# Huber loss on one core: other tile widths, other load pieces, and seven small loads ahead of tile 1

## The chip, the cores and the metric

The kernel runs on 1 core of one Trainium2 chip. The metric is the device time of one execution in microseconds (us). Before the change the median of 3 runs is 1868.01 us (1867.77 to 1872.63). A difference of about 0.3% (5.6 us) is what a measurement of this kernel can tell from no change.

## The reference

Two float32 arrays of 8192 x 8192 go in, one comes out. Every element is computed by itself:

```python
diff = pred - target
abs_diff = np.abs(diff)
return np.where(abs_diff <= 1.0, 0.5 * diff**2, abs_diff - 0.5)
```

The kernel computes it without a branch: with d the difference and c = d clipped to [-1, 1], the result is the larger of c*c/2 and |d| - 0.5. Where |d| is at most 1, the first is at least as large as the second; elsewhere the first is 0.5 and the second is larger.

## The kernel before

The arrays are taken flat and cut into tiles. One tile is a contiguous stretch of 128 times `width` elements, laid over 128 partitions, so that each partition's row is `width` contiguous elements in the memory. There are 524,288 columns to cover. Before the change they are cut into a first tile of 7,616 columns and 39 of W = 13,248, 40 tiles (n = 40) in all.

Four buffers in the on-chip memory hold whole tiles: `a0` and `a1` for `pred`, `b0` and `b1` for `target`. Tile i uses the buffers numbered i mod 2, and the result is made in place in the b buffer and stored from there. So a load of tile i + 2 into a b buffer has to wait until the store of tile i has landed, and a load into an a buffer until the compute of tile i is through with it.

All transfers are issued by one engine, SyncE (SP), in program order, and each is carried by up to 16 DMA engines, which work through what SP has issued. The order is written out by hand: load tile 0, load tile 1, and then for each i compute tile i, store tile i, load tile i + 2. When an instruction on SP waits, all that stands behind it on SP waits as well. Completions are told by eight DMA semaphores taken in turn, so a DMA can also wait for the one that stands eight before it.

`load` (lines 49 to 65) loads most tiles with one DMA for a and one for b. Tiles 0, 1, n-3 and n-2 are loaded in halves, and the last tile in quarters in an order of its own. `store` (67 to 70) stores a tile with one DMA, the last tile with five. `compute` (72 to 100) cuts a tile into pieces: two for tile 0, three of 4,416 columns for most tiles, four for the last but one, eight for the last. Each piece goes through five steps: VectorE subtracts (line 92) and clips (93), ScalarE squares (96) and takes the absolute value (97), and VectorE subtracts 0.5 and takes the larger (86), up to two pieces later.

Of the kernel before, what the change touches and what calls it, by code (L numbers as in the profile page):

```python
# [1 line left out]

# [4 lines left out]

@with_exitstack
def kernel(  # L10
    ctx: ExitStack,
    tc: tile.TileContext,
    pred: bass.AP,
    target: bass.AP,
    out: bass.AP,
):
    nc = tc.nc
    P = 128
    fp32 = mybir.dt.float32
    Alu = mybir.AluOpType  # L20
    Act = mybir.ActivationFunctionType
    SQRT_HALF = 0.70710678118654752

    total = pred.shape[0] * pred.shape[1] // P
    W = 13248
    H, Q, E = W // 2, W // 4, W // 8

    widths = [W] * (total // W)
    if total % W:
        widths.insert(0, total % W)  # L30
    n = len(widths)
    starts = [sum(widths[:i]) * P for i in range(n)]

    def block(x, i):
        flat = x.rearrange("r m -> (r m)")
        return flat[starts[i] : starts[i] + P * widths[i]].rearrange("(p m) -> p m", p=P)

    pool = ctx.enter_context(tc.tile_pool(name="slots", bufs=1))
    a_slots = [pool.tile([P, W], fp32, name=f"a{k}") for k in range(2)]
    b_slots = [pool.tile([P, W], fp32, name=f"b{k}") for k in range(2)]  # L40

    def cuts(pieces):
        at, found = 0, []
        for w in pieces:
            found.append(slice(at, at + w))
            at += w
        return found

    def load(i):
        a, b = a_slots[i % 2], b_slots[i % 2]  # L50

        def get(dst, src, c):
            nc.sync.dma_start(out=dst[:, c], in_=block(src, i)[:, c])  # L53

        if i == n - 1:
            c = cuts([Q] * 4)
            order = [(0, 0), (0, 1), (1, 0), (1, 1), (0, 2), (1, 2), (0, 3), (1, 3)]
            for which, k in order:
                get((a, b)[which], (pred, target)[which], c[k])
            return  # L60
        w = widths[i]
        pieces = [w // 2] * 2 if i in (0, 1, n - 3, n - 2) else [w]
        for c in cuts(pieces):
            get(a, pred, c)
            get(b, target, c)

    def store(i):
        pieces = [Q] * 3 + [E] * 2 if i == n - 1 else [widths[i]]
        for c in cuts(pieces):
            nc.sync.dma_start(out=block(out, i)[:, c], in_=b_slots[i % 2][:, c])  # L70

    def compute(i):
        if i == n - 1:
            pieces = [E] * 8
        elif i == n - 2:
            pieces = [Q] * 4
        elif i == 0:
            pieces = [widths[0] // 2] * 2
        else:
            pieces = [W // 3] * 3  # L80
        todo = []

        def finish(keep):
            while len(todo) > keep:
                a, b = todo.pop(0)
                nc.vector.scalar_tensor_tensor(  # L86
                    out=b, in0=a, scalar=-0.5, in1=b, op0=Alu.add, op1=Alu.max
                )

        for c in cuts(pieces):  # L90
            a, b = a_slots[i % 2][:, c], b_slots[i % 2][:, c]
            nc.vector.tensor_tensor(out=a, in0=a, in1=b, op=Alu.subtract)  # L92
            nc.vector.tensor_scalar(  # L93
                out=b, in0=a, scalar1=-1.0, scalar2=1.0, op0=Alu.max, op1=Alu.min
            )
            nc.scalar.activation(out=b, in_=b, func=Act.Square, scale=SQRT_HALF)  # L96
            nc.scalar.activation(out=a, in_=a, func=Act.Abs)  # L97
            todo.append((a, b))
            finish(2)
        finish(0)  # L100

    ctx.enter_context(tc.manual_schedule())

    load(0)
    load(1)
    for i in range(n):
        compute(i)
        store(i)
        if i + 2 < n:
            load(i + 2)  # L110

# [1 line left out]
_INS = ['pred', 'target']  # L114
_OUTS = [((8192, 8192), 'float32')]

# [23 lines left out]
```

## Time and profile before

| | |
|---|---|
| median of 3 runs | 1868.01 us |
| the profiled execution's own time | 1869.17 us |
| its span | 1867.4 us |
| VectorE (DVE) busy | 1406.2 us, 75% |
| ScalarE (ACT) busy | 903.9 us, 48% |
| DMA queue that SP issues, share of 16 engines | 99.9% |
| bytes moved, mean rate | 805.37 MB, 431 GB/s |
| a load or store of 13,248 columns | 6,624 KB |

The profile shows one execution. The span is what the trace covers, and the execution's own time is a little longer. Busy times are summed per engine. "GB/s" is given for 40 equal slices of the span, 46.7 us each. The queue "q1 hardware_dynamic" is the one that carries all loads and stores; its share of 99.9% says that on average all 16 DMA engines had a packet in hand throughout. A packet is one row of one transfer, carried by one engine, or the 4 bytes with which an engine tells that its part of a transfer is done. In lines of waits, "SPq L53 <- DMA out_dram<-b" reads: SP's queue, at an instruction of line 53, waited for a transfer from a b buffer to the output; then follow total us, times, and the longest. In lines of stretches the columns are the stretch, its length, each engine's busy time with its instructions, the TensorE clock (not used here), the DMA share and GB/s.

### The profile page before, as it was taken

The page shows a single profiled execution, that of the slowest core. Times are in us where ns is not written, and L with a number is a line of the kernel's source. Part 1 is how long each engine was busy: PE and PEld are TensorE (multiplying, and loading weights), DVE is VectorE, ACT ScalarE, POOL GpSimd, SP SyncE. Part 2 cuts the span into 40 slices and gives each one's busy share as a digit, 9 for nine tenths or more (in the row PEclk, how much of TensorE's full clock was granted, in tenths as well). Part 3 has the DMA queues.
Part 4 walks back from the last instruction along what each step waited for, and adds up shares of the span by engine and source line. Part 5 has one row for each costly group of instructions (what it writes and reads, how often), then busy time and mean ns, then how long its engine had stood idle before and what let it go on. Part 6 is the DMA issues. An engine that isn't in the chain of part 4 may idle for free.

```text
span 1867.4 us, 994 instructions
## 1 busy us (share of the span) xinstructions
DVE 1406.2 (75%) x375; ACT 903.9 (48%) x251; POOL 0.2 (0%) x4
## 2 busy tenths in 40 slices
DVE  5677777777777777777777777777777777777886
ACT  3444444444444444444444444444444444444454
POOL 0000000000000000000000000000000000000000
DMA  9999999999999999999999999999999999999999
GB/s 412 423 432 436 436 431 433 436 432 431 428 435 434 435 432 432 432 435 434 434 434 435 432 434 432 435 434 432 436 434 432 434 434 432 432 436 430 432 429 390
DMA packets 19879, 805.37 MB, mean 431 GB/s; under 512 B 2208, under 2 KB 2208, under 8 KB 2464
## 3 DMA queue, kind: packets, MB, share of 16 engines
q1 hardware_dynamic: 19872, 805.32, 99.9%
q14 instruction: 7, 0.06, 0.0%
HBM read 536.87 MB, written 268.44 MB: 431 GB/s over the span
## 4 chain that ended last, share of the span: by engine, by line
DMA 61%; DVE 37%; issue 0%; SPq 0%; DVEq 0%
DMA b<-in_target_dram 33%; DMA out_dram<-b 28%; DVE b L86 15%; DVE a L92 15%; DVE b L93 8%; SPq L53 0%; DVEq L136 0%; DVEq L92 0%
## 5 line engine op out<-in xcount | busy, mean ns | idle before, releaser
L96 ACT ACTIVATE b<-b 128x4416 f32<-128x4416 f32 (+3 forms) x125 | 461.1, 3688 | 945.6 <-DVE b L93 945.6
L92 DVE TENSOR_TENSOR a<-a,b 128x4416 f32<-128x4416 f32 (+3 forms) x125 | 565.4, 4523 | 439.2 <-DMA b<-in_target_dram 439.2
L86 DVE SCALAR_TENSOR_TENSOR b<-a,b 128x4416 f32<-128x4416 f32 (+3 forms) x125 | 558.6, 4521 | 2.7 <-ACT a L97 2.7
L97 ACT ACTIVATE a<-a 128x4416 f32<-128x4416 f32 (+3 forms) x125 | 460.3, 3682 | 0.0
L93 DVE TENSOR_SCALAR b<-a 128x4416 f32<-128x4416 f32 (+3 forms) x125 | 293.1, 2344 | 4.3
L96 ACT ACT_TABLE_LOAD x1 | 1.3, 1283 | 0.7 <-PEq L125 0.7
L125 POOL MEMSET const-bfloat16-1.0<- 128x1 bf16 x1 | 0.1, 102 | 0.0
L125 POOL MEMSET const-uint8-127<- 128x1 uint8 x1 | 0.1, 101 | 0.0
L125 POOL MEMSET const-float32-0.0<- 128x1 f32 x1 | 0.1, 99 | 0.2 <-issue 0.2
L125 POOL MEMSET const-float32-1.0<- 128x1 f32 x1 | 0.1, 98 | 0.0
## 6 DMA issues: line engine op xcount, KB each, us to landing
out_dram<-b SPq DMA_DIRECT2D x38, 6624.0 KB, 26.9
a<-in_pred_dram SPq DMA_DIRECT2D x35, 6624.0 KB, 42.1
b<-in_target_dram SPq DMA_DIRECT2D x35, 6624.0 KB, 31.3
a<-in_pred_dram SPq DMA_DIRECT2D x6, 3312.0 KB, 30.4
b<-in_target_dram SPq DMA_DIRECT2D x6, 3312.0 KB, 30.5
a<-in_pred_dram SPq DMA_DIRECT2D x4, 1656.0 KB, 31.6
b<-in_target_dram SPq DMA_DIRECT2D x4, 1656.0 KB, 18.6
out_dram<-b SPq DMA_DIRECT2D x3, 1656.0 KB, 18.9
```

Source lines behind the costliest of these rows:

```text
L86: nc.vector.scalar_tensor_tensor(out=b, in0=a, scalar=-0.5, in1=b, op0=Alu.add, op1=Alu.max)
L92: nc.vector.tensor_tensor(out=a, in0=a, in1=b, op=Alu.subtract)
L93: nc.vector.tensor_scalar(out=b, in0=a, scalar1=-1.0, scalar2=1.0, op0=Alu.max, op1=Alu.min)
L96: nc.scalar.activation(out=b, in_=b, func=Act.Square, scale=SQRT_HALF)
L97: nc.scalar.activation(out=a, in_=a, func=Act.Abs)
L125: nc = _bacc.Bacc("TRN2", target_bir_lowering=False, num_devices=1)
```

## The change

Four things change.

1. The tile widths. The remainder of 7,616 columns and one full tile are pooled and halved: tile 0 and the last tile have 10,432 columns each, the 38 tiles between them 13,248.
2. The loads of the last tiles. Tile n-3 is loaded whole. Tile n-2 is loaded in pieces of three quarters of a, half of b, one quarter of a, half of b. The last tile takes six loads instead of eight: three quarters of a, then three quarters of b one by one, then the last quarter of a and of b. Tiles 0 and 1 are loaded in halves as before.
3. The pieces of the last tile's compute (eighths) and stores (three quarters and two eighths) stay in number; they shrink with the tile.
4. Seven loads are added among those of tile 0. They read 14, 12, 10, 8, 6, 4 and 2 rows of the first 3,072 columns of tile 1 of `pred` into `a1`, one row out of every eight. Two of them follow the first half of a of tile 0, two the first half of b, three the second half of a. The first load of tile 1 writes the same bytes again later. The number of rows is also the number of DMA engines that such a load is spread over.

On SP, the ninth DMA (the load of 4 rows) now waits for the first one, the tenth and eleventh for the second and third, and the twelfth, the first load of tile 1, for all added loads.

```diff
-    H, Q, E = W // 2, W // 4, W // 8
 
-    widths = [W] * (total // W)
-    if total % W:
-        widths.insert(0, total % W)
+    ends = total % W + W
+    widths = [ends - ends // 2] + [W] * (total // W - 1) + [ends // 2]
...
+    HALVES = (("a", 0, 1), ("b", 0, 1), ("a", 2, 3), ("b", 2, 3))
+    LOADS = {
+        0: HALVES,
+        1: HALVES,
+        n - 2: (("a", 0, 2), ("b", 0, 1), ("a", 3, 3), ("b", 2, 3)),
+        n - 1: (("a", 0, 2), ("b", 0, 0), ("b", 1, 1), ("b", 2, 2), ("a", 3, 3), ("b", 3, 3)),
+    }
+    PARTS = {0: 2, n - 2: 4, n - 1: 8}
...
-    load(0)
-    load(1)
+    def load_all(i):
+        for piece in LOADS.get(i, (("a", 0, 3), ("b", 0, 3))):
+            load(i, *piece)
+
+    EXTRA = 3072
+    later = [14, 12, 10, 8, 6, 4, 2]
+
+    def ahead(count):
+        for _ in range(count):
+            k, r = later[0], len(later)
+            rows = slice(r, r + 8 * (k - 1) + 1, 8)
+            nc.sync.dma_start(
+                out=a_slots[1][rows, :EXTRA], in_=block(pred, 1)[rows, :EXTRA]
+            )
+            later.pop(0)
+
+    for piece, count in zip(LOADS[0], (2, 2, 3, 0)):
+        load(0, *piece)
+        ahead(count)
+    load_all(1)
     for i in range(n):
         compute(i)
         store(i)
         if i + 2 < n:
-            load(i + 2)
+            load_all(i + 2)
```

A piece such as `("a", 0, 2)` names the buffer and the first and last quarter of the tile's columns that the load covers.

More of the change, by code (lines that the diff above doesn't have):

```diff
@@ L40 @@
     b_slots = [pool.tile([P, W], fp32, name=f"b{k}") for k in range(2)]
[L42 to L53, printed above, removed]
-        if i == n - 1:
[L56 to L65, printed above, removed]
@@ L67, in store, with shares, load @@
-    def store(i):
-        pieces = [Q] * 3 + [E] * 2 if i == n - 1 else [widths[i]]
-        for c in cuts(pieces):
+    def shares(i, parts):
+        w = widths[i] // parts
+        edges = [k * w for k in range(parts)] + [widths[i]]
+        return [slice(edges[k], edges[k + 1]) for k in range(parts)]
+    def load(i, which, first, last):
+        quarters = shares(i, 4)
+        c = slice(quarters[first].start, quarters[last].stop)
+        dst, src = (a_slots, pred) if which == "a" else (b_slots, target)
+        nc.sync.dma_start(out=dst[i % 2][:, c], in_=block(src, i)[:, c])
@@ new lines, with store @@
+    HALVES = (("a", 0, 1), ("b", 0, 1), ("a", 2, 3), ("b", 2, 3))
[6 more added lines that the diff above has]
+    PARTS = {0: 2, n - 2: 4, n - 1: 8}
+    def store(i):
+        if i == n - 1:
+            eighths = shares(i, 8)
+            pieces = [slice(eighths[k].start, eighths[k + 1].stop) for k in (0, 2, 4)]
+            pieces += eighths[6:]
+        else:
+            pieces = shares(i, 1)
+        for c in pieces:
@@ L70, in store @@
             nc.sync.dma_start(out=block(out, i)[:, c], in_=b_slots[i % 2][:, c])
     def compute(i):
[L73 to L80, printed above, removed]
         todo = []
@@ L88, in finish @@
                 )
-        for c in cuts(pieces):
+        for c in shares(i, PARTS.get(i, 3)):
             a, b = a_slots[i % 2][:, c], b_slots[i % 2][:, c]
```

## The prediction

> **What bounds the kernel now.** I read the page's busy shares first, then its DMA lines, then SP's waits, then the rate by stretches, and last the single DMA packets in the trace's records.
>
> ```profile
> DVE 1406.2 (75%) x375; ACT 903.9 (48%) x251; POOL 0.2 (0%) x4
> ...
> GB/s 412 423 432 436 436 431 433 436 432 431 428 435 434 435 432 432 432 435 434 434 434 435 432 434 432 435 434 432 436 434 432 434 434 432 432 436 430 432 429 390
> DMA packets 19879, 805.37 MB, mean 431 GB/s; under 512 B 2208, under 2 KB 2208, under 8 KB 2464
> ...
> q1 hardware_dynamic: 19872, 805.32, 99.9%
> ```
>
> The 16 DMA engines are busy for 99.9% of the span, VectorE for 75%, ScalarE for 48%. The rate is level from the third slice to the last but one; only the first and last slices are low. So transfers bound this kernel, and a saving in compute is worth nothing as long as the queue holds work.
>
> ```profile
> SPq L53 <- DMA out_dram<-b: 1000.0, 38, 32.8
> SPq L70 <- DVE b L86: 786.8, 44, 30.8
> ```
>
> The queue that issues everything, SP's, spends nearly the whole span waiting. It waits while transfers issued earlier are still moving, so these waits are cover, not loss: what counts is whether an engine runs dry before SP issues again.
>
> ```profile
> 0.00:25.00 25.00, 9.65 (x3) 7.39 (x3) 0.20 (x4) 1.00 0.95 396
> 49.00:52.00 3.00, 0.00 (x0) 3.00 (x2) 0.00 (x0) 1.00 1.17 397
> 1200.00:1250.00 50.00, 38.53 (x10) 25.81 (x7) 0.00 (x0) 1.00 1.00 434
> 1860.00:1868.00 8.00, 0.00 (x0) 0.00 (x0) 0.00 (x0) 1.00 0.42 173
> ```
>
> The last two columns are the DMA share and GB/s. From 49 to 52 us the engines are fully busy and yet move 397 GB/s instead of 434: packets there take longer. The packet records give the rest. The first packet starts at 1.73 us, the last ends at 1866.06. A row of 52,992 B takes 1956 ns, of 26,496 B 982, of 15,232 B 568, of 13,248 B 495; each engine's share of a DMA closes with a 4-byte packet of 9 ns. With each packet at the shortest time seen for its size, the mean engine needs 1858.6 us; it has 1865.3. Of the 6.7 us between, 3.1 are a few ns on each packet, 0.65 are the first packets of all, and 3.0 are packets that ran over 100 ns long. These 3.0 us lie almost all before 470 us (0.74 at 50 us, 0.45 at 90, 0.57 at 467), mostly at the change from the end of a target load to a store.
>
> Beside this stands the spread of the engines, read off the 16 completions of each DMA: 0.65 us between first and last until 44 us, 1.2 at 156, 2.0 at 297, 3.4 at 501, 3.7 at 1439. Once the engines are over 3 us apart the long packets nearly stop: 0.37 us after 470, against 2.62 between 4 and 470. At the very end it costs: the last engine finishes at 1866.06 and the mean one about 1863.4, so 2.6 us go to the slowest.
>
> **The sum is made against the profiled execution**, 1869.17 us (span 1867.4, 1.8 around it), 1.2 above the median of 1868.01; I add the same change to the median.
>
> **Added bytes.** 14+12+10+8+6+4+2 = 56 rows of 3,072 columns, 12,288 B each: 0.69 MB. Between the 495 ns of 13,248 B and the slope to 568 ns for 15,232 B, a row costs 460 ns and its completion 9. A load of k rows runs on k engines by the change's own words; if these are always the same first ones, two engines carry seven rows (3.3 us), the next two six, and so on to none for the last two. Mean 56 x 0.469 / 16 = +1.6 us. No trace of before shows which engines; were the seven loads on rotating engines, each would carry 1.6.
>
> **Fewer pieces.** DMAs go from 138 to 134 beside the added ones. By the packet sizes, a DMA costs an engine eight rows with some 5 ns each beyond its bytes and one 9 ns completion, of which 3 overlap: four fewer are 4 x (40 + 6) ns, -0.2 us. The bytes of inputs and output are the same.
>
> **The phase of the engines.** The added rows set the engines 0 to 3.3 us apart within the first 30 us, the spread that before reaches after 370 to 470 us. Bounds: at most the 2.62 us of long packets between 4 and 470 us go; at least nothing, and a loss is not excluded, because a pair of engines shares each step. I take -2.0, as the stretch from 300 to 470 us, with 2.0 to 3.0 us of spread, still shows some 1.0 us of long packets, and after 470 they are rare.
>
> **The end.** The last engine is the one that counts. A spread of 3.3 us laid out evenly puts the last 1.65 above the mean, and with the 0.65 us of the start and some drift about 2.3; before has 2.6. I take -0.3; bounds -1.0 (the spread stays as laid out) and +2.0 (natural lag falls on the engines with seven rows).
>
> **The start, covered.** SP now waits: the ninth DMA (4 rows) waits for the first, the tenth and eleventh for the second and third, and the twelfth, the first load of tile 1, for all added rows, since it overwrites them. Behind the twelfth on SP stand the other three loads of tile 1, the store of tile 0 and everything else; VectorE waits for them. A row of 20,864 B takes 775 ns by the slope between 568 and 982, so a half load takes 6.2 us. The first lands near 9 us; the ninth to eleventh are out by about 11, with two half loads (12.4 us) still ahead of the engines. An engine with seven rows finishes the last of them at 2.0 + 0.65 + 3 x 6.2 + 3.3 = 24.6 us. The trace has 0.42 to 0.57 us from a load's last completion packet to the waiting instruction, and 1.0 us from the start of the first issue to the first packet: the twelfth's packets come at about 26.1. An engine with no added rows runs dry at 2.0 + 0.65 + 4 x 6.2 = 27.4. Cover 1.3 us, cost nothing. Were it gone, the engines that stand are those that are 3.3 us ahead, so up to that nothing reaches the end.
>
> **First store, covered.** Tile 0 is 10,432 wide, two pieces of 5,216. Rows by shape give VectorE 4126 ns at 3,808 and 4754 at 4,416, so 5.6 us at 5,216; the scaling goes to 2.9, an activation to 4.5. The last half lands near 31.3; VectorE's subtract and clip (5.6 + 2.9), ScalarE's two (9.0) and the last VectorE step (5.6) end at 54.6. Tile 1's 31.4 us of loads keep the most advanced engine busy until 58.8. Cover some 3 us net of the issue; before had over 10.
>
> **The tail, covered.** Before, VectorE ends its last tile at 1852.5 and transfers run until 1866.06. The last tile shrinks from 13,248 to 10,432 columns, and eight pieces of 1,304 at 4.65 x 1304/1656, about 3.7 us, take 30 instead of 37. Counted from the landing of the store before it, the loads of the last tile keep the queue for 24.6 us, the next store for 15.6, and the last piece is due at 51.0, or 47.7 on the most advanced engine; compute starts at 12.3 and ends at 42.3. Cover some 4 us after the issue; cost nothing.
>
> Sum: +1.6 - 0.2 - 2.0 - 0.3 = **-0.9 us**: span 1866.5, profiled 1868.3, median 1867.1.
>
> [...] The packet records price a DMA's completion at 9 ns on each engine, and 138 DMAs leave the engines 99.9% busy. [...]
>
> **Rivals.**
> 1. *The added rows are simply paid.* The long packets come from something that the phase does not cure, such as the memory's own state early on: all 16 engines are hit at 467 us with 3 us of spread already there, which speaks for it; that they fade as the spread grows speaks against. Then +1.6 - 0.2 + 1.7, by which the two engines with seven rows stand above the mean, = +3.1: 1871.1.
> 2. *The queue runs dry at the start (slower).* Place: the twelfth DMA. The point from which it decides is 3.3 + 1.3 = 4.6 us of delay beyond my 26.1: if the seven loads were each issued only on the landing of the one before, at 0.5 + 1.0 = 1.5 us per round, 10.5 us in all, then 10.5 - 4.6 = 5.9 us stand open, with 3.1 for the paid rows +9.0: 1877.0. For it: the cover of 1.3 is the thinnest of all. Against: each of SP's waits is for a DMA eight back.
> 3. *Reads and writes mixed across the engines slow them.* If each change of direction ran 3.3 us at 397 instead of 434 GB/s, three changes in each of 39 tiles cost 117 x 3.3 x 0.085 = 33 us: 1901. Against: from 500 us on the engines already are 3.4 to 3.7 us apart, at 434.
> 4. *Much faster.* Even with every early long packet gone and all engines ending together the gain is 2.6 + 2.6 + 0.2 - 1.6 = 3.8: 1864.2, short of 0.3%.
>
> **Chances.** Forecast (between 1865 and 1869) 0.52; rows simply paid (1869 to 1873) 0.27; dry at the start 0.10; mixed 0.03; close to the floor, or below it by scatter of the runs, 0.08. A measurement of this kernel can tell about 0.3%, 5.6 us, from no change: the forecast, the paid rows and most of the fourth lie within it; of the 0.10 for a dry start some 0.06 lie beyond 1873.6, with the 0.03 and 0.04 of the paid rows, where runs scatter upward as one of the three before did (1872.63). Faster by that much 0.05, from the fourth, same 0.82, slower 0.13. The range goes from the fourth case to the upper end of the second: 1864.0 to 1873.0.
>
> **What would show it.** Right: completions of one DMA spread some 3.3 to 4 us already in the first 60 us; the slice rates near 434 from the second slice on; packets over 100 ns long below 1.5 us in sum after the first ones; no engine idle at 27 and 58 us; the last transfer ends 13 us after VectorE. Wrong: long packets as before (the phase is no cure), a slice below 400 near 27 us (dry), or more spread at the end than 4 us.

## The result, and the profile after

The changed kernel takes 1872.10 us (median of 20 runs, 1871.70 to 1873.08), the kernel before 1868.42 (20 runs, 1867.39 to 1872.63). The ratio is 1.0019, with a 95% interval of 1.0013 to 1.0025: slower by 3.7 us. That lies within the 0.3% that the prediction gave 0.82, but on the other side of no change than the forecast of -0.9 us. It also lies in the band from 1869 to 1873 that the prediction gave to its first rival, with 0.27.

The page after, its parts on busy time, rate and DMA queue:

```profile
DVE 1406.0 (75%) x375; ACT 903.8 (48%) x251; POOL 0.2 (0%) x4
...
GB/s 385 437 434 435 433 432 434 432 434 435 431 434 435 435 433 433 433 434 434 433 433 435 431 434 435 434 433 434 434 433 435 432 433 435 433 432 434 431 430 382
DMA packets 19416, 806.06 MB, mean 431 GB/s; under 512 B 2201, under 2 KB 2201, under 8 KB 2457
...
q1 hardware_dynamic: 19408, 806.00, 99.8%
```

The first of the 40 slices fell from 412 to 385 GB/s, and the second rose from 423 to 437. The whole difference of the change stands at the two ends of this line: a worse first slice (27 GB/s less over 46.8 us are 1.26 MB, 2.9 us at 433 GB/s), a better second one, and 382 instead of 390 in the last (the kernel without the added loads, below, has 381 there and is not slower). Between these ends both kernels have 433 GB/s in the mean.

The stretches of the changed kernel (columns: stretch, length, busy time of each engine, TensorE clock, DMA share, GB/s) show where, the last two columns above all:

```profile
0.00:25.00 25.00, 6.38 (x2) 1.28 (x1) 0.20 (x4) 1.00 0.94 355
8.00:12.00 4.00, 0.00 (x0) 0.00 (x0) 0.00 (x0) 1.00 0.99 299
16.00:19.00 3.00, 0.42 (x1) 0.00 (x0) 0.00 (x0) 1.00 1.10 331
24.00:28.00 4.00, 3.05 (x2) 0.88 (x1) 0.00 (x0) 1.00 1.05 365
49.00:52.00 3.00, 0.46 (x1) 2.51 (x1) 0.00 (x0) 1.00 1.02 442
56.00:62.00 6.00, 5.97 (x3) 0.00 (x0) 0.00 (x0) 1.00 1.04 442
1200.00:1250.00 50.00, 38.52 (x11) 25.82 (x8) 0.00 (x0) 1.00 1.00 434
```

The kernel before, in the first of these short stretches:

```profile
8.00:12.00 4.00, 0.00 (x0) 0.00 (x0) 0.00 (x0) 1.00 1.01 434
```

The added loads move in three groups, near 9, 17 and 25 us, and at each of them the engines are fully busy at 299 to 365 GB/s: slow, and not empty. The slow stretch that the kernel before had at 49 to 52 us (397 GB/s), just ahead of the packets of its first store, is gone (442), as forecast; in the changed kernel these packets begin at 62.3 us, and the six us ahead of them run at 442 as well.

The packet records say the same by size. The 56 added rows of 12,288 B took 719 ns in the mean (median 759, 460 to 1036), not 460. Rows of the half loads beside them, 775 ns at their shortest, took up to 1554 near 9 us. Packets over 100 ns longer than the shortest of their size, in us per engine:

| | first ones | 4 to 31 us | 31 to 470 us | after 470 us |
|---|---|---|---|---|
| before | 0.65 | 0.00 | 2.61 | 0.37 |
| after | 0.61 | 2.93 | 0.18 | 0.14 |

Of the 2.93 us between 4 and 31 us, 0.9 are in the added rows themselves and 2.0 in the rows of the large loads.

SP's waits of the changed kernel in its first 45 us show the two new ones:

```profile
SPq L49 <- DMA a<-in_pred_dram: 15.8, 4, 8.3
SPq L105 <- DMA a<-in_pred_dram: 4.3, 2, 4.0
```

L49 is where tile loads are issued, L105 the added loads. The wait of the twelfth DMA ended at 28.1 us, 3.0 later than reckoned, yet in no microsecond between 3 and 60 us did as much as 0.2 of the 16 engines stand without a packet. So the waits cost nothing that the trace shows; slow rows did.

### The profile page after: what moved, and what is told of

Read it like the earlier page. It is cut to its first block, busy times and chain, and to the rows that moved or that the text cites. A ratio compares the mean times of both kernels' runs of the same rounds, so it can differ in the third digit from the quotient of the medians.

```text
span 1870.3 us, 995 instructions
## 1 busy us (share of the span) xinstructions
DVE 1406.0 (75%) x375; ACT 903.8 (48%) x251; POOL 0.2 (0%) x4
## 4 chain that ended last, share of the span: by engine, by line
DMA 62%; DVE 37%; issue 0%; DVEq 0%; SPq 0%
DMA b<-in_target_dram 33%; DMA out_dram<-b 28%; DVE b L76 15%; DVE a L82 15%; DVE b L83 8%; DMA a<-in_pred_dram 1%; SPq L49 0%; DVEq L144 0%; DVEq L82 0%
```

## The experiments

All twelve start from the changed kernel, except the one called "only added". Times are medians, and each ratio is against runs of the kernel before that were taken with it: median 1868.42 for the changed kernel, 1868.34 for eight apart and neighbours with 35 rows, third of a row and half rows, 1868.06 or 1868.08 for the others. So differences of some 0.3 us between rows of the table can come from that alone. "Rows" are the added rows of 12,288 B (in two runs shorter); "long" are the packets over 100 ns too long, us per engine.

| run | time, us | ratio to before, 95% interval | rows: median, longest, ns | long 4 to 31 us | long 31 to 470 us |
|---|---|---|---|---|---|
| changed kernel | 1872.10 | 1.0013 to 1.0025 | 759, 1036 | 2.93 | 0.18 |
| no added loads | 1868.52 | 0.9994 to 1.0012 | none | 0.05 | 2.05 |
| partitions nine apart | 1870.70 | 1.0005 to 1.0023 | 614, 851 | 1.70 | 0.29 |
| rows read nine apart | 1871.71 | 1.0012 to 1.0029 | 728, 932 | 2.72 | 0.11 |
| equal bytes | 1870.33 | 1.0003 to 1.0021 | none | 0.04 | 1.19 |
| neighbouring partitions | 1885.52 | 1.0079 to 1.0107 | 708, 1212 | 2.39 | 2.39 |
| four apart | 1869.53 | 0.9999 to 1.0017 | 460, 487 | 0.08 | 1.00 |
| four apart, moved up | 1870.24 | 1.0002 to 1.0020 | 498, 607 | 1.17 | 0.56 |
| eight apart, 35 rows | 1871.97 | 1.0010 to 1.0028 | 578, 945 | 2.11 | 0.38 |
| neighbours, 35 rows | 1875.19 | 1.0022 to 1.0047 | 1021, 1638 | 5.41 | 1.51 |
| four apart, third of a row | 1869.09 | 0.9996 to 1.0014 | 159, 186 | 0.05 | 1.35 |
| half rows | 1869.39 | 0.9999 to 1.0016 | 234, 408 | 1.06 | 0.38 |
| only added | 1873.36 | 1.0017 to 1.0040 | 732, 1011 | 2.79 | 1.32 |

Three theories stood at the start. P: it is the partitions written, eight apart, that make the added rows slow. H: it is the rows read, eight apart in the main memory, that do. B: only the bytes and the waits count, or the recut tiles. The expectations say "ports" for what partitions would share by theory P; that there is such a thing was the author's assumption, and no run shows it.

**No added loads.**

```diff
-    later = [14, 12, 10, 8, 6, 4, 2]
+    later = []
...
-    for piece, count in zip(LOADS[0], (2, 2, 3, 0)):
+    for piece, count in zip(LOADS[0], (0, 0, 0, 0)):
```

> The changed kernel without the seven added loads: the recut tiles and pieces alone. If the added loads carry the whole loss, this stands with the kernel before at 1868.2 us (four DMAs fewer, -0.2), and packets over 100 ns long return between 30 and 470 us (2 to 3 us per engine in sum), while those between 4 and 31 us are gone. If the recut (a tile 0 and a last tile of 10,432 columns, other pieces) carries a part, it stands above 1869.5.

The time stands with the kernel before: the recut and the fewer pieces are worth nothing that these runs can tell. The long packets after 31 us are back (2.05). So the loss comes with the added loads: 3.6 us between the two medians, 3.2 with each beside its own runs of the kernel before.

**Where the rows are written, where they are read.**

```diff
+            to = slice(r, r + 9 * (k - 1) + 1, 9)
             rows = slice(r, r + 8 * (k - 1) + 1, 8)
             nc.sync.dma_start(
-                out=a_slots[1][rows, :EXTRA], in_=block(pred, 1)[rows, :EXTRA]
+                out=a_slots[1][to, :EXTRA], in_=block(pred, 1)[rows, :EXTRA]
```

P's figures stand first, then those of H and B.

> The added loads read the same rows, eight apart, but write them to partitions nine apart (overwritten later, as before). [...] Then a row takes 460 to 520 ns instead of some 890, the 2.9 us of long packets between 4 and 31 us fall below 0.8, and the time is 1869.2 to 1870.2. Theory H (the rows read, eight apart in the main memory, meet there): no difference to the changed kernel, 1871.6 to 1872.6, rows at some 890 ns. Theory B (only the added bytes and waits count): 1871.6 to 1872.6 as well.

The other run keeps `to` eight apart and reads `rows` nine apart.

> The added loads read rows nine apart and write them to partitions eight apart. Theory P: as the changed kernel, rows at some 890 ns, 2.9 us of long packets between 4 and 31 us, 1871.6 to 1872.6. Theory H: rows at 460 to 520 ns and 1869.2 to 1870.2. Theory B: 1871.6 to 1872.6.

Reading other rows changed little (2.72 against 2.93 us of long packets, rows at 728 ns). Writing other partitions took 1.2 us of long packets and 1.4 us of time away. H falls. P is only half confirmed: the rows came to 614 ns, not to 460 to 520, and the time to 1870.7, above the 1869.2 to 1870.2 that P gave. Whether a choice of partitions exists that brings the rows to 460, later runs test.

**Equal bytes.**

```diff
     for piece, count in zip(LOADS[0], (2, 2, 3, 0)):
         load(0, *piece)
-        ahead(count)
+        if count == 3:
+            nc.sync.dma_start(out=a_slots[1][:, :1344], in_=block(pred, 1)[:, :1344])
```

> In place of the seven loads one load of 128 rows of 1,344 columns, the same 688,128 bytes, 43,008 on each of the 16 engines: the bytes are paid, but no engine is set apart from another. By my sum's terms: +1.6 for the bytes, -0.2 for fewer DMAs, no cure of the long packets between 30 and 470 us (2 to 3 us return), none of those between 4 and 31: 1869.8. Theory B: 1871.6 to 1872.6, as the changed kernel.

1870.33 is 1.8 us above the run without added loads, near the +1.6 of the sum. B falls as far as bytes go: the same bytes on all engines alike cost half of what the seven loads cost. Its waits are not the same here; that they are not the cause is shown by the runs in which the destination alone differs, further down, which keep them. The runs scatter more here (1869.11 to 1872.52), and the later long packets were 1.19 where 2 to 3 were expected.

**Neighbouring partitions: a test that tested something else.**

```diff
+            to = slice(r, r + 1 * (k - 1) + 1, 1)
...
-                out=a_slots[1][rows, :EXTRA], in_=block(pred, 1)[rows, :EXTRA]
+                out=a_slots[1][to, :EXTRA], in_=block(pred, 1)[rows, :EXTRA]
```

> As the changed kernel, but the added rows are written to neighbouring partitions (14 rows to partitions 7 to 20, 12 to 6 to 17, and so on). [...] Rival S (a small load on fewer than 16 engines is slow in itself, whatever it writes): rows and time as in the changed kernel, 1871.6 to 1872.6.

17.5 us slower, far above what S gave and above P's estimate of 1873.5 to 1877, and not for slower rows: their median is 708 ns, against 759 in the changed kernel. The seven loads now write partitions 7 to 20, 6 to 17, 5 to 14 and so on, which overlap, so each waits on SP for the landing of the one before: six waits, 31.8 us. SP's waits of this kernel in the first 45 us (L106 is the added loads' line here):

```profile
SPq L106 <- DMA a<-in_pred_dram: 31.8, 6, 9.5
```

And three stretches of it:

```profile
9.00:12.00 3.00, 0.00 (x0) 0.00 (x0) 0.00 (x0) 1.00 0.01 0
20.00:24.00 4.00, 2.88 (x1) 0.00 (x0) 0.00 (x0) 1.00 0.43 93
31.00:37.00 6.00, 0.00 (x0) 6.00 (x2) 0.00 (x0) 1.00 0.12 32
```

In the first stretch nothing moved at all. Between 3 and 60 us each of the 16 engines stood for 11.9 us in the mean. This is the second rival of the prediction, made by accident, at about twice its price: it had 5.9 us of standing and +9.0 in all. It did not happen in the changed kernel.

**The destination alone.** Three runs (four apart; eight apart, 35 rows; neighbours, 35 rows) with the same seven loads of 8 to 2 rows, 35 in place of 56, and the same rows read; the destination alone differs, and no partition is written twice. Beside them stands one (four apart, moved up) in which every row, read and written, is moved up by four partitions.

```diff
-    later = [14, 12, 10, 8, 6, 4, 2]
+    later = [8, 7, 6, 5, 4, 3, 2]
...
-            rows = slice(r, r + 8 * (k - 1) + 1, 8)
+            first = r % 4 + 32 * (r // 4)              # four apart; + 4: moved up
+            rows = slice(first, first + 4 * (k - 1) + 1, 4)
+            to = rows
+            to = slice(r, r + 8 * (k - 1) + 1, 8)      # eight apart
+            to = slice(8 * r, 8 * r + k)               # neighbours
```

Of the three lines for `to`, each run has one; four apart and four apart, moved up, write `rows` itself, which is the same as the first. The expectations follow in the order four apart ("own ports" in their words), moved up, eight apart, neighbours. The two cases of the second are rows at 460 ns and rows at some 890.

> [...] Theory P: no two engines share a port, every row takes 460 ns, long packets between 4 and 31 us stay below 0.3; 35 x 0.469 / 16 = +1.0 us of bytes over the kernel without added loads (1868.5), of which the cure of later long packets gives back a part: 1868.3 to 1869.8. Rival S: rows above 600 ns, 1870 or more.

> [...] Theory P: rows between the two cases, 500 to 750 ns as with partitions nine apart (median 614), long packets between 4 and 31 us 0.4 to 1.2; 1869 to 1870.5. Rival S: the same as with own ports.

> [...] Theory P: a row takes 850 to 910 ns in the larger loads instead of 460, long packets between 4 and 31 us rise from 0.1 to 1.5 or more, time 0.7 to 2 us above the run with own ports (1870.2 to 1871.5). If it is not the ports, rows stay at 460 and the time at 1869.5.

> [...] Theory P: rows up to some 1800 ns (four times 452), long packets between 4 and 31 us 2.5 or more, time 1871 to 1873.5; as the two largest loads follow each other, the engines that carry them all slow alike. If it is not the ports, 460 ns and 1869.5.

The stretches of the three groups of added loads, first with partitions four apart:

```profile
8.00:12.00 4.00, 0.00 (x0) 0.00 (x0) 0.00 (x0) 1.00 1.01 432
16.00:19.00 3.00, 2.40 (x1) 0.00 (x0) 0.00 (x0) 1.00 1.08 463
24.00:28.00 4.00, 1.11 (x1) 2.86 (x1) 0.00 (x0) 1.00 1.06 451
```

With partitions eight apart:

```profile
8.00:12.00 4.00, 0.00 (x0) 0.00 (x0) 0.00 (x0) 1.00 1.03 359
16.00:19.00 3.00, 1.55 (x1) 0.00 (x0) 0.00 (x0) 1.00 0.99 295
24.00:28.00 4.00, 1.96 (x1) 2.01 (x1) 0.00 (x0) 1.00 1.05 398
```

With neighbouring partitions:

```profile
8.00:12.00 4.00, 0.00 (x0) 0.00 (x0) 0.00 (x0) 1.00 0.98 208
16.00:19.00 3.00, 0.00 (x0) 0.00 (x0) 0.00 (x0) 1.00 1.17 333
24.00:28.00 4.00, 3.61 (x2) 0.32 (x1) 0.00 (x0) 1.00 1.15 373
```

Read the last column downward from fence to fence: 432, 359, 208 GB/s in the first group, with the engines as busy; without added loads it is 433. The longest rows go 487, 945, 1638 ns, near one, two and three and a half times 460; in the two largest loads with neighbouring partitions, seven of 15 rows took 1408 to 1513. The times go 1869.53, 1871.97, 1875.19, that is +2.4 and +5.7 (+2.2 and +5.4 with each beside its own runs of the kernel before), next to +2.0 and +5.3 us of long packets between 4 and 31 us. Loads, bytes, rows read and waits are the same in the three, so neither H nor B has a part in these differences. With partitions four apart the 35 rows took 460 to 487 ns, 461 in the mean, so a small load on few engines is not slow in itself, and the rival S falls. Four apart, moved up, lies between (498 ns, 385 GB/s in the first group), as P expected, somewhat faster in the rows and at the upper end in time. Eight apart came out above its range by 0.5 us, neighbours, 35 rows, by 1.7. The factor of four in P's 1800 ns was the author's assumption and is not shown: the longest row there took 1638 ns.

What these partitions share, no run shows; the runs show that the choice of the partitions alone sets this price, 487, 945 or 1638 ns for the longest row and 1869.53, 1871.97 or 1875.19 us in all.

**Dose.**

```diff
-    EXTRA = 3072
+    EXTRA = 1536        # half rows; 1024 with four apart: third of a row
```

> The changed kernel with added rows of 1,536 instead of 3,072 columns, to the same partitions. If the loss goes with the bytes and the shared ports, about half of it stays: bytes +0.8, long packets between 4 and 31 us 1.2 to 1.7, time 1869.8 to 1870.6. If it goes with the seven loads as such (issue, completion, waits), 1871.5 to 1872.5.

> The run with own ports with rows of 1,024 instead of 3,072 columns: the bytes cost 0.36 us instead of 1.0 in the mean and 1.1 instead of 3.3 on the engines with seven rows; the lower eight engines are set 0 to 1.1 us apart. If a small spread already cures the long packets between 31 and 470 us (below 1.2 in sum, against 2.05 without added loads), the time is 1867.3 to 1868.3, the best so far; if it does not, 1868.3 to 1869.3.

Half rows kept 0.9 of the 3.6 us, less than the half expected: most rows of the first two loads took the shortest time, 234 ns, and long packets between 4 and 31 us were 1.06. A third of a row on partitions four apart stayed at 159 to 186 ns a row, but 1.1 us of spread, as reckoned, cured little (1.35 us left of 2.05), and the time, 1869.09, is not below that of the kernel without added loads. None of the twelve beat the kernel before.

**Only added.** The kernel before with the seven loads put into its own tile 0.

```diff
-    load(0)
...
+    load(0, (2, 2, 3, 0), ahead)
     load(1)
```

The lines by which `load` and `ahead` issue them are left out.

> The kernel before, with the seven loads of the change put among those of its tile 0 (7,616 columns) and nothing else changed. If the recut is worth nothing, this loses what the change loses: long packets between 4 and 31 us near 2.9, time 1871.5 to 1873. The half loads of tile 0 are 4.5 us instead of 6.2, so the first load of tile 1, which waits for all added rows, leaves SP near 24 us, when the engines without added rows have been dry for some 2 us. If that wait costs at the end, the time is above 1873; if the engines that are ahead absorb it, not.

1873.36, 0.4 above the upper end, with 2.79 us of long packets between 4 and 31 us, nearly as in the changed kernel. The engines hardly stood (0.07 us each near 23 us) where 2 us on the foremost had been expected: the slow rows delayed them as much as the waiting load. The 1.3 us above the changed kernel is not separated from it, since the intervals overlap (1.0017 to 1.0040, and 1.0013 to 1.0025). But the trace has a candidate: 1.32 us of long packets after 31 us instead of 0.18, nearly all of them just ahead of the first store's packets, although the completions of one DMA were 2.3 us apart by then:

```profile
53.00:57.00 4.00, 0.00 (x0) 4.00 (x2) 0.00 (x0) 1.00 1.02 301
```

## Why the prediction was wrong

The account of the two profiled executions, per engine: bytes and pieces, each packet at its shortest time, +1.4 us, long packets between 4 and 31 us +2.9, between 31 and 470 us -2.4, after 470 us -0.2, a few ns on each packet +0.4: +2.1, and the mean engine's end moved from 1863.5 to 1865.5. The last engine stands 3.3 us above the mean instead of 2.6: +0.7. The execution's own time went from 1869.17 to 1872.03, +2.9; the medians differ by 0.8 more because the profiled execution before stood 0.75 above its median and the one after did not.

- **What bounds the kernel** was right: transfers, with the engines busy throughout.
- **Added bytes, +1.6.** Right as bytes: "equal bytes" measured +1.8. The step that failed is the next sentence of that part, "a row costs 460 ns and its completion 9". The price came from rows of transfers over 128 partitions; the run with partitions four apart pays it, but the change writes partitions eight apart. There the rows took 719 ns in the mean, 0.9 us per engine more than reckoned, and the rows of the large loads beside them were stretched by another 2.0: 2.9 us that the sum had at nothing, enough to turn -0.9 into +2.0. The larger part is thus not the added rows' own price but what they did to their neighbours, for which the sum had no term. It gave no upper bound for either, and none of the four rivals named them.
- **Fewer pieces, -0.2.** Without added loads the kernel measured 1868.52 against 1868.08: no difference to be told, as expected of 0.2.
- **The phase of the engines, -2.0.** Near in size: -2.4 against before, -1.9 against the kernel without added loads (2.05 to 0.18), and the completions of one DMA were 2.7 to 3.2 us apart from 34 to 65 us, near the 3.3 asked for. That the phase is what does it is likely but not shown: "only added", 2.3 us apart, kept 1.32, half rows, 1.6 apart, kept 0.38, and equal bytes, not set apart, had 1.19 instead of 2.05. Rival 1, for which the long packets stay, came near with 1871.1 by luck: it left out both the slow rows (+2.9) and the long packets that went (-2.4).
- **The end, -0.3.** It was +0.7, within the bounds of -1.0 to +2.0. But the kernel without added loads also has 3.4, so the added rows need not be what moved it; the runs give 2.6 to 4.5 in no order that I can explain.
- **The start, the first store, the tail, at nothing:** right; between 3 and 1850 us an engine stood for 0.13 us in the mean. The twelfth DMA came 3.0 us late, for the slow rows, and the engines that it serves were as late; the first store left at 57.2 us instead of 54.6, still in time.
- **A fixed price for each DMA**, beside rows and completions, was not in the sum, and none of note shows: with partitions four apart the seven added DMAs cost 1.0 us over no added loads, all in all.

Two of its own signs of being wrong showed: a stretch below 400 GB/s near 27 us (365), though not from a dry queue, and 5.1 us instead of at most 4 between the first and last engine at the end (4.2 before).

With the row price corrected, the sum would have been -0.9 + 2.9 = +2.0. The rest of the 3.7 is the end (+1.0 against the forecast), what the phase and the small packets gave or took (-0.4 - 0.2 + 0.4), and the 0.8 by which the profiled execution before stood off its median.

Not tried: setting all 16 engines apart with every row at 460 ns. With partitions four apart no added load has more than 8 rows, and which partitions would give loads of up to 14 rows that price, no run shows. So what the phase is worth by itself on all engines was not measured.

## What to carry to other kernels

The price of a small transfer could not be read here from rows of a large one (719 ns in the mean for 460): see which partitions it writes, bound its rows by what other partitions gave here (up to 945 and 1638 ns for 460), and count the rows of the transfers beside it, which lost twice as much (2.0 us against 0.9). Where the rate in a stretch falls while the DMA share stays at 1 (299 GB/s at 0.99 here), packets are slow and not missing; compare them by size. A small load that a later load overwrites also sets waits on the issuing queue (the twelfth DMA left at 28.1 us), and one that overlaps the load before it can cost more than all its bytes (11.9 us of standing here, against the 1.8 of equal bytes).

## What was not expected of the hardware

- Destination partitions alone changed a load's rows from 460 ns to 945 and 1638, with the same bytes and source rows on as many engines (8 to 2 for each load).
- The completions of 4 bytes suffered too: 9.0 ns in the mean between 3 and 32 us with partitions four apart, 12.2 in the changed kernel, 15.3 with neighbouring partitions and 35 rows.
- Engines that start within 0.65 us of each other pay 1.2 to 2.6 us in long packets between 31 and 470 us (before, no added loads, equal bytes), mostly ahead of stores, until they have drifted some 3 us apart (3.4 at 501 us before, with 0.37 us of long packets after 470). Where all were set apart the changed kernel and three others paid 0.1 to 0.4, but "only added" 1.3; where at most eight were, it was 0.4 to 1.5. What these packets wait for, no run here shows.
